# A layer's modulation vectors as fused dot products on VectorE, placed behind SwiGLU blocks

## The chip, the core and the metric

The kernel runs on one core of a Trainium2 chip. A core has five engines that run side by side and wait for each other by semaphores: TensorE (matrix products into PSUM), VectorE (DVE, elementwise work and reductions), ScalarE (ACT, functions and copies), GpSimd (POOL, elementwise work on SBUF) and SyncE (SP), which here issues the transfers from HBM. Each engine takes its instructions strictly in the order in which they stand in its queue. The metric is the time of one execution on the device in microseconds (us); less is better.

## What is computed

The reference is a backbone of two layers over 256 context tokens and 256 latent tokens of width 1024. In both layers a vector of six modulation terms (shift, scale and gate of the mixer and of the feed-forward) scales what goes in and out. It is a product of a weight matrix with the silu of a conditioning vector, once for the context (`c_ctx`) and once for the latents (`c`):

```python
mod_lat = (jax.nn.silu(c) @ ada_w[l] + ada_b[l])[:, None, :]
mod_ctx = (jax.nn.silu(c_ctx) @ ada_w[l] + ada_b[l])[None, None, :]
sh_m, sc_m, g_m, sh_f, sc_f, g_f = jnp.split(mod_lat, N_MOD, axis=-1)
...
hc = modulate(rmsnorm(ctx_s, norm_mix_g[l]), csh_m, csc_m)
yc, hf_c, hb_c = mix(l, hc @ w_in[l], False, None, None)
ctx_s = ctx_s + cg_m * yc
hcf = modulate(rmsnorm(ctx_s, norm_ffn_g[l]), csh_f, csc_f)
ctx_s = ctx_s + cg_f * channel_mix(l, hcf)
```

`mix` is three kinds of sequence mixers (Fourier, Hyena, S5 state space). `channel_mix` is a dense SwiGLU of width 2816 in layer 0, `(silu(h @ w_gate) * (h @ w_up)) @ w_down`, and in layer 1 eight SwiGLU experts of width 3584, of which each token takes two. All is float32.

## The kernel before

The program runs through these stages in order: mixers of layer 0 (to about 295 us); the output projection `outp` with the norm behind it (to about 385 us); the dense feed-forward of layer 0 (to about 800 us); mixers of layer 1; router and experts of layer 1, whose 336 weight loads of 1 MB make up the second half of the time. A scheduler sets each engine's order when the kernel is built, from the order of the code, the dependencies, free buffers and a timing model; nothing is reordered on the chip.

**Modulation (`ada`, L429).** A modulation vector has 6 x 1024 entries, that is 48 columns `m` of 128. Column `m` needs 128 rows of the transposed weights, `ar` (128 x 1024, 512 KB, loaded at L432 from `adaT` into a ring of two buffers), and the row `crow` that holds silu of the conditioning vector on all partitions. The entry is the dot product of the two along the free axis, for `s` = 0 (context) and `s` = 1 (latents). There are two ways: one fused instruction on VectorE (`'v'`, L437, output `jk`, the sum as its accumulator), or a product on GpSimd (`'g'`, L440, into `pd`, one buffer) and a copy with accumulation on ScalarE (L441). When eight columns are there, `mods_done` adds the bias and forms the gains `G` (L384, L387). Columns 0 to 31 of layer 0 are made elsewhere, on TensorE. Columns 32 to 47 of layer 0 are asked for ahead of the output projection (L1155 to L1158): 8 dots on VectorE, 24 on GpSimd and ScalarE. All 48 of layer 1 are asked for by `ahead(fi)` (L1243), eight columns at the end of each feed-forward step, all on GpSimd and ScalarE; from column 16 on only for the latents. That is 88 products on GpSimd and 8 fused dots.

**Weight split (`load` L185, `split` L191, L192).** Every float32 weight block goes into a ring of two buffers `raw`, then into a high half `wh` (copy on ScalarE, L191) and a low half `wl` (difference on VectorE, L192), each 128 x 1024 and in a ring of two. TensorE then does three products a block: high by high, high by low, low by high.

**Feed-forward.** Six steps of up to four blocks of 128 SwiGLU values (22 in all). A block has a gate and an up product of 24 matmuls each, of 512 columns (`pgu`); then silu on ScalarE (L1283), the product `hv` on VectorE (L1285), its high half `HH` on ScalarE (L1286) and its low half `HL` on VectorE (L1287). After the second block of a step the down products of the step before stand (`downs`): eight of up to 12 matmuls into two accumulators `pacc`, each added to the residual stream by two VectorE instructions `xT` of 256 columns (L1227). In steps 1 to 5 `mats1` builds the six sets of S5 matrices of layer 1 by the table `MATS1` (`s5_mats`, L558 and on: products and sums on VectorE and GpSimd, transposes `pbt` on TensorE, stores to HBM), for the mixers of layer 1.

**Output projection.** `outp` (L1161) is eight products whose results `xT` takes up (L1169); the norm sums squares (`nac`, L516), and `put` makes the feed-forward's input in halves `fhH` and `fhL` (L536 to L538).

SP issues all of these loads in one queue; one that waits for a free buffer holds those behind it.

Of the kernel before, what the change touches and what calls it, by code (L numbers as in the profile page):

```python
# [8 lines left out]
F32 = mybir.dt.float32  # L9
F32R = mybir.dt.float32r  # L10
I32 = mybir.dt.int32
AF = mybir.ActivationFunctionType
# [4 lines left out]
D = 1024  # L17
# [8 lines left out]
S5_OFF = 1408  # L26
NHY = [2, 2, 2, 2, 2, 1]
NHY0 = [2,2,2,2,1,2]
MATS1 = [(), (0,), (1,), (2, 3), (4,), (5,)]
HYO = [[10, 2, 3, 4, 5, 6, 7, 8, 9, 0, 1], [2, 3, 4, 5, 6, 7, 8, 9, 10, 0, 1]]  # L30
OW = 5
NRAW = 15
# [103 lines left out]
def build(tc, A, out, dbg=None, upto='all'):  # L136
    nc = tc.nc
    V, S, G, PE, SP = nc.vector, nc.scalar, nc.gpsimd, nc.tensor, nc.sync
    tt_, ts_, stt, act = V.tensor_tensor, V.tensor_scalar, V.scalar_tensor_tensor, S.activation
    gtt = G.tensor_tensor  # L140
    mul, add, sub = OP.mult, OP.add, OP.subtract
# [15 lines left out]
    par = es_par.enter_context(tc.tile_pool(name="par", bufs=1, side="right"))  # L157
# [50 lines left out]
    crow = par.tile([128, 2, D], F32, name="crow")  # L208
# [217 lines left out]
        mods_done(0, 4 * c, 4)  # L426


    def ada(l, m0, m1, eng, pool):  # L429
        for m in range(m0, m1):  # L430
            r = pool.tile([128, D], F32, name="ar", tag="ar", bufs=2)
            SP.dma_start(r, A['adaT'][l, m])  # L432
            for s in range(1 if l == 1 and m >= 16 else 0, 2):
                o = mods[l][:, m, s:s + 1]
                if eng(m, s) == 'v':
                    jk = par.tile([128, D], mybir.dt.bfloat16, name="jk", tag="jk", bufs=1)
                    stt(jk, r, 1.0, crow[:, s], op0=mul, op1=mul, accum_out=o)  # L437
                else:
                    pd = par.tile([128, D], F32, name="pd", tag="pd", bufs=1)
                    gtt(pd, r, crow[:, s], op=mul)  # L440
                    act(pd, pd, AF.Copy, accum_out=o)  # L441
            if m % 8 == 7:
                mods_done(l, m - 7, 8, 1 if l == 1 and m >= 16 else 0)

# [113 lines left out]
    def s5_mats(p, l, q, M, rh, rd):  # L558
# [24 lines left out]
        bh = lambda v: v[:, :, None, :].to_broadcast(sh)  # L583
        for i, (src, op) in enumerate(((bre, sub), (bim, add))):
            tt_(src, bt(PB[0]), bh(bb[:, i]), op=mul)
            (tt_ if l else gtt)(x2, bt(PB[1]), bh(bb[:, 1 - i]), op=mul)
            tt_(src, src, x2, op=op)
            pt = pt_('mat', (128, 4, 128), "pbt")
            for g in range(4):
                PE.transpose(pt[:, g], src[:, g].rearrange("p t h -> p (t h)"), ident)  # L590
            act(M[:, :, 128 * i:128 * i + 128], pt, AF.Copy)
# [535 lines left out]
    with z_es:  # L1127
        yH = z.tile([128, KD, 512], F32R, name="yH", tag="hH")
        yL = z.tile([128, KD, 512], F32R, name="yL", tag="hL")

        with tc.tile_pool(name="z0p", bufs=1) as z2, tc.tile_pool(name="ada0", bufs=1) as p_:
            def fill0(q):
                if q == 0:
                    ada_ring(4, p_)
                if q == 1:
                    ada_ring(5, p_)
                if q == 3:
                    ada_ring(6, p_)
                if q == 4:
                    ada_ring(7, p_)  # L1140
            mixers(0, hH, hL, z2, yH, yL, fill0)
        tap('yH0', yH.bitcast(F32))
        tap('yL0', yL.bitcast(F32))
        rx_es, xp = ExitStack(), ExitStack()
        rx = rx_es.enter_context(tc.tile_pool(name="rx", bufs=1))
        xpool = xp.enter_context(tc.tile_pool(name="xpool", bufs=1))
        xT = xpool.tile([128, KD, 512], F32, name="xT")
        for q in range(4):
            SP.dma_start(xT[:, 2 * q:2 * q + 2], A['xT'][:, 2 * q:2 * q + 2])
        fh = xp.enter_context(tc.tile_pool(name="fh", bufs=1))  # L1150
        fhH, fhL = (fh.tile([128, KD, 512], F32R, name=n_) for n_ in ("fhH", "fhL"))
        ac = rx.tile([128, 2, D], F32, name="nac", tag="xtok")
        nrm = [Norm(0, 1, xT, s, ac[:, s, 0:256]) for s in range(2)]
        apl = xp.enter_context(tc.tile_pool(name="ada1", bufs=1))
        ada(0, 32, 36, lambda m, s: 'gv'[s], apl)  # L1155
        ada(0, 36, 40, lambda m, s: 'gv'[s], apl)
        ada(0, 40, 44, lambda m, s: 'gg'[s], apl)
        ada(0, 44, 48, lambda m, s: 'gg'[s], apl)  # L1158
        with tc.tile_pool(name="ow", bufs=OW) as ow:

            def outp(m, ws, s0, s1):  # L1161
                n = 256 * (s1 - s0)
                cs_ = slice(256 * s0, 256 * s1)
                pa = pacc((128, n))
                for k in (0, 1, 5, 6, 7, 2, 3, 4):
                    mm3(pa, ws[0][:, k], ws[1][:, k], yH[:, k, cs_], yL[:, k, cs_], k == 0, k == 4)
                for s in range(s0, s1):
                    x = xT[:, m, 256 * s:256 * s + 256]
                    stt(x, pa[:, 256 * (s - s0):256 * (s - s0) + 256], mods[0][:, 16 + m, s:s + 1], x, op0=mul, op1=add)  # L1169
                    nrm[s].feed(m)  # L1170
            raws, ws = {}, {}

            def wget(m):
                c = m // 2
                if c not in raws:
                    raws[c] = load(wcols(A['w_out'][0], 256 * c, 256), KD, 256)
                return split(raws[c][:, :, (m % 2) * 128:(m % 2) * 128 + 128], KD, 128,
                             *([ow] if m >= KD - OW else []))
            for m in range(KD - OW):
                outp(m, wget(m), 0, 2)  # L1180
            for m in range(KD - OW, KD):
                ws[m] = wget(m)
                outp(m, ws[m], 0, 1)
            nrm[0].stats()
            nrm[0].put(lambda k: fhH[:, k, 0:256], lambda k: fhL[:, k, 0:256])
            for m in range(KD - OW, KD):
                outp(m, ws[m], 1, 2)
            nrm[1].stats()
            nrm[1].put(lambda k: fhH[:, k, 256:512], lambda k: fhL[:, k, 256:512])
# [10 lines left out]
    with tc.tile_pool(name="ffn", bufs=2, side="right") as fp, banks(gu=3, fk=1):  # L1200
# [9 lines left out]
        def mats1(q):  # L1210
            M = pp1.tile([128, 4, 768], F32, name="M")
            rh = pp1.tile([128, 4, 64], F32, name="rh")
            s5_mats(pp1, 1, q, M, rh, rdr[q])
            SP.dma_start(rhdr[q], rh)
            SP.dma_start(mdr[q][:, :, 0:512], M[:, :, 0:512])
            SP.dma_start(mdr[q][:, :, 640:768], M[:, :, 640:768])
# [23 lines left out]
                        down(g, 4 * dh + 2 * q + m, w, m * 128, 0, 2)  # L1240


        def ahead(fi):  # L1243
            ada(1, 8 * fi, 8 * fi + 8, lambda m, s: 'g', apl)
            for q in MATS1[fi]:
                mats1(q)
        pend = None
        for fi, f0 in enumerate(range(0, nff, 4)):
            nf = min(4, nff - f0)
# [2 lines left out]
            for c in range(0, nf, 2):  # L1252
# [18 lines left out]
                for m in range(2):  # L1271
# [12 lines left out]
                    hv = tmp.tile([128, 512], F32, name="hv", tag="t512b", bufs=2)  # L1284
                    tt_(hv, sg, pp[1], op=mul)  # L1285
                    act(HH[:, c + m], hv, AF.Copy)  # L1286
                    tt_(HL[:, c + m], hv, HH[:, c + m].bitcast(F32), op=sub)  # L1287
                if pend:
                    downs(pend)
                    pend = None  # L1290
            ahead(fi)
            pend = f0, nf, HH, HL

        ac = apl.tile([128, D], F32, name="nac", tag="ar", bufs=2)
# [536 lines left out]
```

## Time and profile before

| | us |
|---|---|
| median of three runs (1838.38 to 1842.83) | 1841.52 |
| the profiled execution | 1841.73 |
| its span, first to last instruction | 1839.8 |
| of it busy: TensorE | 1714.5 (93%) |
| VectorE | 805.9 (44%) |
| GpSimd | 518.4 (28%) |
| ScalarE | 429.4 (23%) |

The profile is of one execution. Its span is 1.9 us short of that execution's time, and the execution is 0.2 us from the median. Busy TensorE includes pipelined matmuls whose ends are modelled, so they overlap: the distance between two starts tells the pace. An idle time is put down to the instruction whose semaphore came last.

### The profile page before, as it was taken

The page shows a single profiled execution, that of the slowest core. Times are in us where ns is not written, and L with a number is a line of the kernel's source. Part 1 is how long each engine was busy: PE and PEld are TensorE (multiplying, and loading weights), DVE is VectorE, ACT ScalarE, POOL GpSimd, SP SyncE. Part 2 cuts the span into 40 slices and gives each one's busy share as a digit, 9 for nine tenths or more (in the row PEclk, how much of TensorE's full clock was granted, in tenths as well). Part 3 has the DMA queues.
Part 4 walks back from the last instruction along what each step waited for, and adds up shares of the span by engine and source line. Part 5 has one row for each costly group of instructions (what it writes and reads, how often), then busy time and mean ns, then how long its engine had stood idle before and what let it go on. Part 6 is the DMA issues. An engine that isn't in the chain of part 4 may idle for free. (4 is left out here: it accounts for less than half of the span.)

```text
span 1839.8 us, 47195 instructions
## 1 busy us (share of the span) xinstructions
PE 1714.5 (93%) x20825; PEld 1193.8 (65%) x20825; DVE 805.9 (44%) x1502; ACT 429.4 (23%) x776; POOL 518.4 (28%) x512
## 2 busy tenths in 40 slices
PE   7988899899998998999998999999999989999984
PEld 4665667867766776788777656666666656666642
DVE  7589968875776667363853001111111101011102
ACT  4332324455444443232231000000000000000001
POOL 5965535567877676000420000000000000000000
PEclk7998999999999999999998999999999999999998
DMA  8244345434557555354649999999999999999994
GB/s 297 87 116 126 94 148 177 144 106 145 168 180 248 190 194 194 120 162 141 191 150 419 405 394 418 419 420 419 419 419 418 419 419 419 418 413 413 412 419 160
DMA packets 145461, 506.80 MB, mean 275 GB/s; under 512 B 18590, under 2 KB 71648, under 8 KB 101216
## 3 DMA queue, kind: packets, MB, share of 16 engines
q1 hardware_dynamic: 145248, 503.70, 72.0%
q8 instruction: 165, 2.70, 0.6%
q14 instruction: 48, 0.39, 0.1%
HBM read 489.34 MB, written 14.32 MB: 274 GB/s over the span
## 5 line engine op out<-in xcount | busy, mean ns | idle before, releaser
L148 PE MATMUL pgu<-raw,xe 128*32 128x256 f32 x9408 | 528.2, 379 | 12.2 <-DMA raw<-in_mwp_dram 11.4
L148 PEld LDWEIGHTS pgu<-raw,xe 128*32 128x32 f32 x9408 | 316.3, 110 | 209.5 <-DMA raw<-in_mwp_dram 15.1
L1652 DVE TENSOR_TENSOR sg<-sg,pgu 128x384 f32<-128x384 f32 (+1 forms) x56 | 28.2, 504 | 629.8 <-ACT sg L1651 629.8
L148 PE MATMUL py<-raw,hT 128*32 128x256 f32 x4704 | 270.0, 379 | 8.3 <-DMA raw<-in_mwp_dram 8.2
L440 POOL TENSOR_TENSOR pd<-ar,crow 128x1024 f32<-128x1024 f32 x88 | 226.6, 2575 | 105.4 <-ACT pd L441 83.9
L1547 POOL TENSOR_TENSOR ob<-ob,fgb 128x512 f32<-128x512 f32 x1 | 1.3, 1262 | 880.4 <-ACT ob L1546 880.4
L148 PEld LDWEIGHTS py<-raw,hT 128*32 128x32 f32 x4704 | 156.0, 110 | 110.4 <-DMA raw<-in_mwp_dram 7.9
L192 DVE TENSOR_TENSOR wl<-raw,wh 128x1024 fp32r<-128x1024 f32 x95 | 169.2, 1783 | 72.4 <-ACT wh L191 70.5
L1651 ACT ACTIVATE sg<-pgu 128x384 f32<-128x384 f32 (+1 forms) x56 | 25.2, 450 | 705.6 <-PE pgu L148 705.6
L148 PE MATMUL pgu<-fhL,wh 128*128 128x512 f32 (+1 forms) x376 | 146.2, 389 | 5.1 <-DVE fhL L538 5.1
L148 PE MATMUL pgu<-fhH,wh 128*128 128x512 f32 (+1 forms) x392 | 147.6, 387 | 1.4 <-ACT sg L1283 0.8
L148 PE MATMUL pgu<-fhH,wl 128*128 128x512 f32 (+1 forms) x360 | 142.1, 396 | 3.3 <-DVE wl L192 3.3
L191 ACT ACTIVATE wh<-raw 128x1024 fp32r<-128x1024 f32 x95 | 99.9, 1054 | 147.1 <-PE pacc L148 67.3
L441 ACT ACTIVATE pd<-pd 128x1024 f32<-128x1024 f32 x88 | 93.0, 1057 | 123.9 <-POOL pd L440 121.1
L148 PE MATMUL pacc<-HH,wh 128*128 128x512 f32 (+1 forms) x192 | 76.8, 401 | 14.2 <-DVE xT L1227 10.0
L148 PEld LDWEIGHTS pgu<-fhL,wh 128*128 128x128 f32 x376 | 72.2, 192 | 22.9 <-DVE fhL L538 6.4
L148 PEld LDWEIGHTS pgu<-fhH,wh 128*128 128x128 f32 x392 | 74.0, 193 | 16.6 <-issue 1.1
L148 PEld LDWEIGHTS pgu<-fhH,wl 128*128 128x128 f32 x360 | 68.1, 189 | 23.0 <-issue 4.7
L148 PE MATMUL pacc<-HL,wh 128*128 128x512 f32 (+1 forms) x192 | 74.6, 389 | 0.0
L148 PE MATMUL pacc<-HH,wl 128*128 128x512 f32 (+1 forms) x192 | 73.7, 390 | 0.3 <-DVE wl L192 0.3
L148 PE MATMUL pacc<-h,wm 128*128 128x256 f32 x272 | 64.5, 391 | 1.2 <-ACT h L549 1.2
L148 PEld LDWEIGHTS pacc<-h,wm 128*128 128x128 f32 x272 | 51.5, 194 | 9.0 <-ACT h L549 1.4
(583 smaller groups left out, 2410.8 us busy)
## 6 DMA issues: line engine op xcount, KB each, us to landing
raw<-in_mwp_dram SPq DMA_DIRECT2D x336, 1024.0 KB
ar<-in_adaT_dram SPq DMA_DIRECT2D x64, 512.0 KB
raw<-in_fwg_dram SPq DMA_DIRECT2D x11, 1024.0 KB
raw<-in_fwu_dram SPq DMA_DIRECT2D x11, 1024.0 KB
raw<-in_fwd_dram SPq DMA_DIRECT2D x11, 1024.0 KB
raw<-in_adaN_dram SPq DMA_DIRECT2D x8, 1024.0 KB
ar<-in_adaN_dram SPq DMA_DIRECT2D x16, 512.0 KB
raw<-in_w_out_dram SPq DMA_DIRECT2D x8, 1024.0 KB
```

The source lines that it names most:

```text
L148: return PE.matmul(o, l, r, start=start, stop=stop, **kw)
L191: act(h, r, AF.Copy)
L192: tt_(l, r, h.bitcast(F32), op=sub)
L440: gtt(pd, r, crow[:, s], op=mul)
L441: act(pd, pd, AF.Copy, accum_out=o)
L1547: gtt(o_, o_, fgb[:, hs], op=mul)
L1651: act(sg[:, 0:n], p[:, 0:n, 0:128], AF.Silu)
L1652: tt_(sg[:, 0:n], sg[:, 0:n], p[:, 0:n, 128:256], op=mul)
```

## The change

All 96 dots now are fused instructions on VectorE; `pd`, its product on GpSimd and its sum on ScalarE are gone. Ahead of the output projection only columns 32 to 39 of layer 0 are left (16 dots). The others go through the list `AHEAD`: 20 entries of four dots (two columns for both `s`, or four columns for the latents), one entry behind each of the first 20 `HL`. `tc.issue_after` gives each dot of an entry an edge from that `HL`, so that VectorE's queue has them behind it; their loads are free of it. `jk` moves to the pool that holds `ar`. In layer 1's matrix building the product `x` (L586) goes from VectorE to GpSimd, as it already stands in layer 0, and `MATS1` moves the fourth matrix (number 3) from step 3 to step 4.

```diff
--- before.py
+++ after.py
@@ -26,7 +26,7 @@
 S5_OFF = 1408
 NHY = [2, 2, 2, 2, 2, 1]
 NHY0 = [2,2,2,2,1,2]
-MATS1 = [(), (0,), (1,), (2, 3), (4,), (5,)]
+MATS1 = [(), (0,), (1,), (2,), (3, 4), (5,)]
 HYO = [[10, 2, 3, 4, 5, 6, 7, 8, 9, 0, 1], [2, 3, 4, 5, 6, 7, 8, 9, 10, 0, 1]]
 OW = 5
 NRAW = 15
@@ -426,19 +426,13 @@
         mods_done(0, 4 * c, 4)
 
 
-    def ada(l, m0, m1, eng, pool):
+    def ada(l, m0, m1, pool):
         for m in range(m0, m1):
             r = pool.tile([128, D], F32, name="ar", tag="ar", bufs=2)
             SP.dma_start(r, A['adaT'][l, m])
             for s in range(1 if l == 1 and m >= 16 else 0, 2):
-                o = mods[l][:, m, s:s + 1]
-                if eng(m, s) == 'v':
-                    jk = par.tile([128, D], mybir.dt.bfloat16, name="jk", tag="jk", bufs=1)
-                    stt(jk, r, 1.0, crow[:, s], op0=mul, op1=mul, accum_out=o)
-                else:
-                    pd = par.tile([128, D], F32, name="pd", tag="pd", bufs=1)
-                    gtt(pd, r, crow[:, s], op=mul)
-                    act(pd, pd, AF.Copy, accum_out=o)
+                jk = pool.tile([128, D], mybir.dt.bfloat16, name="jk", tag="jk", bufs=1)
+                stt(jk, r, 1.0, crow[:, s], op0=mul, op1=mul, accum_out=mods[l][:, m, s:s + 1])
             if m % 8 == 7:
                 mods_done(l, m - 7, 8, 1 if l == 1 and m >= 16 else 0)
 
@@ -583,7 +577,7 @@
         bh = lambda v: v[:, :, None, :].to_broadcast(sh)
         for i, (src, op) in enumerate(((bre, sub), (bim, add))):
             tt_(src, bt(PB[0]), bh(bb[:, i]), op=mul)
-            (tt_ if l else gtt)(x2, bt(PB[1]), bh(bb[:, 1 - i]), op=mul)
+            gtt(x2, bt(PB[1]), bh(bb[:, 1 - i]), op=mul)
             tt_(src, src, x2, op=op)
             pt = pt_('mat', (128, 4, 128), "pbt")
             for g in range(4):
@@ -1152,10 +1146,7 @@
         ac = rx.tile([128, 2, D], F32, name="nac", tag="xtok")
         nrm = [Norm(0, 1, xT, s, ac[:, s, 0:256]) for s in range(2)]
         apl = xp.enter_context(tc.tile_pool(name="ada1", bufs=1))
-        ada(0, 32, 36, lambda m, s: 'gv'[s], apl)
-        ada(0, 36, 40, lambda m, s: 'gv'[s], apl)
-        ada(0, 40, 44, lambda m, s: 'gg'[s], apl)
-        ada(0, 44, 48, lambda m, s: 'gg'[s], apl)
+        ada(0, 32, 40, apl)
         with tc.tile_pool(name="ow", bufs=OW) as ow:
 
             def outp(m, ws, s0, s1):
@@ -1240,10 +1231,14 @@
                         down(g, 4 * dh + 2 * q + m, w, m * 128, 0, 2)
 
 
-        def ahead(fi):
-            ada(1, 8 * fi, 8 * fi + 8, lambda m, s: 'g', apl)
-            for q in MATS1[fi]:
-                mats1(q)
+
+        AHEAD = [(0, m, m + 2) for m in range(40, 48, 2)] + [(1, m, m + 2) for m in range(0, 16, 2)]
+        AHEAD += [(1, m, m + 4) for m in range(16, 48, 4)]
+
+        def ahead(ins):
+            if AHEAD:
+                with tc.issue_after(ins.ins):
+                    ada(*AHEAD.pop(0), apl)
         pend = None
         for fi, f0 in enumerate(range(0, nff, 4)):
             nf = min(4, nff - f0)
@@ -1284,11 +1279,12 @@
                     hv = tmp.tile([128, 512], F32, name="hv", tag="t512b", bufs=2)
                     tt_(hv, sg, pp[1], op=mul)
                     act(HH[:, c + m], hv, AF.Copy)
-                    tt_(HL[:, c + m], hv, HH[:, c + m].bitcast(F32), op=sub)
+                    ahead(tt_(HL[:, c + m], hv, HH[:, c + m].bitcast(F32), op=sub))
                 if pend:
                     downs(pend)
                     pend = None
-            ahead(fi)
+            for q in MATS1[fi]:
+                mats1(q)
             pend = f0, nf, HH, HL
 
         ac = apl.tile([128, D], F32, name="nac", tag="ar", bufs=2)
```

VectorE's queue from the second-last block ahead of a down stage (step 3) into that stage. Before; `HL` ends a block, `wl` is a weight split, `xT` the evictions of down products, `bb`, `u`, `bre` the matrix building:

```order
L1287 TENSOR_TENSOR HL<-hv,HH 128x512
L192 TENSOR_TENSOR wl<-raw,wh 128x1024
L1285 TENSOR_TENSOR hv<-sg,pgu 128x512
L192 TENSOR_TENSOR wl<-raw,wh 128x1024
L1287 TENSOR_TENSOR HL<-hv,HH 128x512
L1227 SCALAR_TENSOR_TENSOR xT<-pacc,mods_100,xT 128x256 x4
L245 TENSOR_TENSOR bb<-u_5919,u_5920 128x64
L246 TENSOR_TENSOR u_5919<-bs,wim 128x64
L247 TENSOR_TENSOR u_5920<-bs,wre 128x64
```

The same place in the change, with its own line numbers:

```order
L1282 TENSOR_TENSOR HL<-hv,HH 128x512
L435 SCALAR_TENSOR_TENSOR jk,mods_101<-ar,crow 128x1024 x2
L192 TENSOR_TENSOR wl<-raw,wh 128x1024
L435 SCALAR_TENSOR_TENSOR jk,mods_101<-ar,crow 128x1024 x2
L1280 TENSOR_TENSOR hv<-sg,pgu 128x512
L192 TENSOR_TENSOR wl<-raw,wh 128x1024
L1282 TENSOR_TENSOR HL<-hv,HH 128x512
L435 SCALAR_TENSOR_TENSOR jk,mods_101<-ar,crow 128x1024
L1218 SCALAR_TENSOR_TENSOR xT<-pacc,mods_100,xT 128x256 x2
L435 SCALAR_TENSOR_TENSOR jk,mods_101<-ar,crow 128x1024
L1218 SCALAR_TENSOR_TENSOR xT<-pacc,mods_100,xT 128x256 x2
L245 TENSOR_TENSOR bb<-u_6320,u_6321 128x64
```

Two dots stand on each side of a weight split inside a block, and in the down stage one dot stands ahead of each pair of evictions.

SP's queue around the down weights of step 4. Before (`ar` are the modulation loads, `md` the stores of built matrices, `cs` and `bs` parameters for them):

```order
L185 DMA raw<-in_fwg_dram 128x8x256
L432 DMA ar<-in_adaT_dram 128x1024
L185 DMA raw<-in_fwu_dram 128x8x256
L432 DMA ar<-in_adaT_dram 128x1024 x3
L567 DMA cs<-in_s5c_dram 128x2x64
L566 DMA bs<-in_s5b_dram 128x2x64
L616 DMA rd_132<-R 4x32x240
L568 DMA d_6451<-in_s5d_dram 128x1x16
L432 DMA ar<-in_adaT_dram 128x1024
L185 DMA raw<-in_fwd_dram 128x4x512
```

In the change:

```order
L185 DMA raw<-in_fwg_dram 128x8x256
L185 DMA raw<-in_fwu_dram 128x8x256
L432 DMA ar<-in_adaT_dram 128x1024 x6
L185 DMA raw<-in_fwd_dram 128x4x512
L432 DMA ar<-in_adaT_dram 128x1024 x2
L185 DMA raw<-in_fwd_dram 128x4x512
L432 DMA ar<-in_adaT_dram 128x1024 x4
L185 DMA raw<-in_fwg_dram 128x8x256
```

Six modulation loads now stand between an up weight and the down weight behind it, where there were four.

## Rows read from the trace of the kernel before

**Rows 1.** Page, part 1: busy us, share of the span, instructions.
```profile
PE 1714.5 (93%) x20825; PEld 1193.8 (65%) x20825; DVE 805.9 (44%) x1502; ACT 429.4 (23%) x776; POOL 518.4 (28%) x512
```

**Rows 2.** Stretches: length, busy us (count) by engine, clock, DMA share, GB/s.
```profile
295.00:385.00 90.00, 76.20 (x494) 68.65 (x494) 80.88 (x122) 47.01 (x84) 48.66 (x19) 0.92 0.51 166
385.00:750.00 365.00, 341.66 (x1621) 258.51 (x1620) 248.73 (x272) 165.53 (x269) 258.05 (x156) 0.97 0.56 181
750.00:830.00 80.00, 78.99 (x431) 63.81 (x430) 40.60 (x91) 26.58 (x47) 0.52 (x1) 0.98 0.48 152
950.00:1840.00 890.00, 844.47 (x15134) 531.46 (x15133) 137.88 (x329) 58.58 (x126) 1.55 (x2) 0.98 0.98 401
```

**Rows 3.** Chain that ended last: start us, us, what (two of its loads).
```profile
950.41 5.20 DMA raw<-in_w_out_dram
...
1797.22 19.66 DMA raw<-in_mwp_dram
```

**Rows 4.** Waits, matmuls in 295 to 385: releaser, us, times, longest.
```profile
PE pgu L148 <- DVE fhL L538: 5.1, 6, 1.4
PE pacc L148 <- DVE xT L1169: 3.3, 2, 2.0
...
PE pacc L148 <- DVE wl L192: 1.7, 1, 1.7
```

**Rows 5.** Waits, matmuls in 385 to 750, whole list.
```profile
PE pacc L148 <- DVE xT L1227: 10.0, 5, 3.8
PE pbt L590 <- DVE bre L587: 5.0, 2, 3.2
PE pacc L148 <- ACT M L591: 4.1, 2, 3.1
PE pgu L148 <- DVE wl L192: 3.3, 3, 1.6
PE pbt L590 <- DVE bim L587: 0.8, 1, 0.8
```

**Rows 6.** Groups of VectorE in 295 to 385: busy us, mean ns, idle before.
```profile
L192 DVE TENSOR_TENSOR wl<-raw,wh 128x1024 fp32r<-128x1024 f32 x10 | 19.3, 1946 | 2.2 <-ACT wh L191 2.2
L538 DVE SCALAR_TENSOR_TENSOR fhL<-nf,mods,fhH 128x256 fp32r<-128x256 f32 x16 | 16.6, 1055 | 0.0
```

**Rows 7.** Groups of VectorE in 385 to 750.
```profile
L192 DVE TENSOR_TENSOR wl<-raw,wh 128x1024 fp32r<-128x1024 f32 x52 | 107.0, 2058 | 49.6 <-ACT wh L191 48.9
...
L1287 DVE TENSOR_TENSOR HL<-hv,HH 128x512 fp32r<-128x512 f32 x18 | 20.4, 1133 | 1.7 <-ACT HH L1286 1.7
...
L586 DVE TENSOR_TENSOR x<-PB,bb 128x512 f32<-128x512 f32 x12 | 11.5, 956 | 0.1
```

**Rows 8.** Groups of VectorE in 750 to 800.
```profile
L192 DVE TENSOR_TENSOR wl<-raw,wh 128x1024 fp32r<-128x1024 f32 x9 | 11.0, 1226 | 12.9 <-ACT wh L191 12.5
L1227 DVE SCALAR_TENSOR_TENSOR xT<-pacc,mods,xT 128x256 f32<-128x256 f32 x8 | 3.5, 480 | 5.8 <-PE pacc L148 5.8
L1287 DVE TENSOR_TENSOR HL<-hv,HH 128x512 fp32r<-128x512 f32 x4 | 2.7, 684 | 0.0
L1285 DVE TENSOR_TENSOR hv<-sg,pgu 128x512 f32<-128x512 f32 x3 | 2.1, 689 | 12.1 <-PE pgu L148 12.1
```

**Rows 9.** Tiles pd and jk: ns min/median/max, first and last start.
```profile
L440 POOL TENSOR_TENSOR pd<-ar,crow x88: 2346/2400/3391, 293.9 to 721.6; 128x1024 f32<-128x1024 f32 x88
...
L437 DVE SCALAR_TENSOR_TENSOR jk<-ar,crow x8: 1208/1213/3053, 293.6 to 331.0; 128x1024 bf16<-128x1024 f32 x8
```

**Rows 10.** Timeline, one product on GpSimd and VectorE's next: start us, us.
```profile
521.53 2.84 POOL L440 TENSOR_TENSOR pd<-ar,crow 128x1024 f32<-128x1024 f32 x1
...
522.04 2.88 DVE L1287 TENSOR_TENSOR HL<-hv,HH 128x512 fp32r<-128x512 f32 x1
```

**Rows 11.** Timeline, TensorE inside a gate product.
```profile
576.70 0.39 PE L148 MATMUL pgu<-fhL,wh 128*128 128x512 f32 x1
...
577.40 0.40 PE L148 MATMUL pgu<-fhL,wh 128*128 128x512 f32 x1
```

## Prediction, written before the change was run

> **What bounds the kernel now.** I read the page first: TensorE is busy 93% of the span, VectorE 44%, GpSimd 28% [rows 1]. Such shares are averages over stages, so the next view is the table of stretches [rows 2]. From 950 us on, the transfers are busy for 0.98 of the time: the experts' weights set the pace there, and the chain that ended last runs through these loads to the end [rows 3]. Nothing in the change touches that part. It ends a fixed time after it starts, so a microsecond saved ahead of it is a microsecond of the result, and none of it is hidden by a later wait.
>
> The change works on two stretches ahead of that. In 295 to 385 us (output projection and the norm behind it) TensorE is busy 76.20 of 90 us at a mean granted clock of 0.92, while VectorE is busy 80.88 [rows 2]. In 385 to 750 us (dense feed-forward) TensorE is busy 341.66 of 365 us at 0.97 [rows 2]. So TensorE bounds both, and what can be won is what it loses there: idle 13.8 and 23.3 us, and clock (1 - 0.92) x 90 = 7.2 and (1 - 0.97) x 365 = 11.0 us. Together that is 55 us. The clock is at its lower level, 1.2 instead of 2.4 GHz, only in short pieces of these stretches.
>
> Next I read who ends TensorE's idle time. In the first stretch VectorE ends 5.1 + 3.3 + 1.7 = 10.1 of the 13.8 us [rows 4]. In the second it is the eviction of the down products (10.0), the matrix building (5.0), a ScalarE copy (4.1) and the low half of a weight split (3.3): 22.4 of 23.3 us [rows 5]. VectorE is not full in the second stretch (248.73 of 365 us, rows 2), so the question is why it is late. The groups of its instructions answer that: the split `wl` takes 2058 ns on average in the feed-forward [rows 7], but 1226 ns in 750 to 800 us, where GpSimd is idle [rows 8, 2]; `HL` takes 1133 against 684 ns [rows 7, 8]. A pair of rows shows the mechanism: GpSimd begins a product `pd` at 521.53 for 2.84 us, VectorE's `HL` begins at 522.04 and lasts 2.88 us instead of 0.68 [rows 10]. A VectorE instruction with two operands in SBUF stands still until GpSimd's product is through. The 88 products `pd` are what GpSimd mostly does [rows 9].
>
> **What is removed.** All 88 products on GpSimd at a median of 2.40 us, and the 88 ScalarE sums behind them [rows 9]. GpSimd's own time is on no path to the end, but its hold on VectorE is. In the feed-forward `wl` gets back 52 x (2058 - 1226) = 43 us and `HL` 18 x (1133 - 684) = 8 us [rows 7, 8]. In the first stretch `wl` gets back 10 x (1946 - 1226) = 7.2 us, and `fhL` 16 x (1055 - 480) = 9.2 us, with the 128x256 form of `xT` as its clean price [rows 6, 8]. The ScalarE sums also go; in the ACT queue they stand ahead of the copies that the weight split and `HH` need, and I take the 4.1 us put down to a ScalarE copy [rows 5] to be of that kind. The twelve `x` products of the matrix building leave VectorE as well (11.5 us, rows 7) and go to GpSimd, at about 1.2 us each (an estimate: half of `pd`'s 2.40 us for half its columns). There they hold VectorE for about 14 us, in place of 88 products of 2.40 us.
>
> **What is added.** 88 more dot products on VectorE. The eight that it already does give the price: 1.21 us at the median, 3.05 at worst behind a GpSimd product [rows 9]. In the first stretch eight more cost 9.7 us, and `wl` and `fhL` alone give back 16.4: VectorE ends 6.7 us lighter there or better. In the feed-forward 80 dots cost 97 us against 43 + 8 + 11.5 = 62.5 from these groups and more from the small ones, so its load stays near 250 to 285 of some 350 us. What changes is where the time stands. Four dots follow one `HL`. A block of SwiGLU values is 48 matmuls, and three matmuls take 0.70 us [rows 11], so a block is 11.2 us; VectorE's work in it is then two `wl` (2.45), `hv` (0.69), `HL` (0.68) and four dots (4.85): 8.7 us [rows 8, 9]. It fits, and the order puts a `wl` between the dots, so in the gate and up blocks I cost the dots at nothing; their cover is the 2.5 us that VectorE has over, and without it each group would cost up to 4.9 us.
>
> In the down stage the cover is thinner. There the order has a dot ahead of the first pair of evictions and another ahead of the second, and the matrix building among them. Two accumulators serve eight down products, so a product waits when the eviction two before it is late by more than its own 2.8 us (12 matmuls). I price a late dot and a late 128x512 instruction, 1.21 + 0.68 [rows 8, 9]: about 2 us for each of the five down stages, 10 us in all. The bound below is nothing, and the bound above is four dots a stage, 24 us.
>
> **The other queues.** The `ar` loads still go through SP in a ring of two, and now wait for dots in place of GpSimd products. Behind them in the same queue stand the weight loads `fwg`, `fwu`, `fwd`, the stores of the built matrices and the small parameter loads. A dot group frees its two buffers within 2.4 us of its start, and a 1 MB load lands in 5.20 us [rows 3]; a block is 11.2 us. So I cost this wait at nothing; the second rival says what it is worth otherwise. `MATS1` builds the fourth matrix one step later, with the fifth; it still ends before the next layer's mixers, nothing.
>
> **The sum.** First stretch: of the 10.1 us that VectorE ends I take back all but 2, since the dots stand in front of the first evictions there: 8, and half of the clock's 7.2, 3.6. That is 11.6 us, between 0 and 21. Feed-forward: 22.4 us of named waits go and 10 come, a gain of 12.4 us; idle time falls from 23.3 to 10.9 us, and with the clock's loss in proportion (11.0 to 5.2) there are 5.8 more. That is 18.2 us, between 0 and 34. The profiled execution took 1841.73 us (span 1839.8), level with the median of 1841.52: 1841.7 - 11.6 - 18.2 = 1811.9, so **1812 us**.
>
> **Rivals.** *All of it goes*: no dot is ever in the way, and 55.3 us vanish: 1786 us. The 8.7 of 11.2 us speak for it, the evictions behind dots against it. Chance 0.12.
>
> *Half of it*: the first stretch gains its 11.6 us, and in the feed-forward the dots in front of evictions and splits cost as much as the GpSimd products did: 1830 us. For it speaks that VectorE's load there hardly falls. Chance 0.16.
>
> *Nothing*: this happens as well, and in the first stretch the 16 dots wait in VectorE's queue for their `ar` loads, with splits and evictions behind them: 1841 us. Chance 0.08.
>
> *Slower, by the load queue*: in the later steps up to six `ar` loads stand in SP between one weight load and the next, and each waits for a dot that itself waits for an `HL`. If in each of ten half steps one weight load is late by a landing of 5.20 us [rows 3], that adds 52 us: 1864 us. It decides from 3 us per half step, where the 30 us gained are gone. Against it: before, the same ring waited for GpSimd with the same loads behind, and no weight load of the feed-forward is among TensorE's releasers [rows 5]. Chance 0.09.
>
> *Slower, by a dot at half rate*: if a dot with its accumulator took twice the 1.21 us, a block would need 3.8 + 9.7 = 13.5 us of VectorE for 11.2 of TensorE, and 20 blocks x 2.3 = 47 us would come on top: 1859 us. The eight rows at 1.21 us, level with `wl` at 1.23 for as many elements, speak against it [rows 8, 9]; they ran apart, not four in a row. Chance 0.03. The Trainium skill (Vector Engine (DVE) Microarchitecture Reference, Points that are easy to get wrong) has this as a rule: a scalar_tensor_tensor with two SBUF sources that are not bf16 runs at half its throughput, as no read port is left for the accumulator. By that rule the dots would bind as this rival says; the trace of before does not agree with it.
>
> **How the numbers follow.** The forecast, 1800 to 1824 us, has 0.52. This kernel's measurement can tell some 0.3%, 5.5 us, from no change. Faster by more than that (under 1836): 0.52 + 0.12 + 0.16 = 0.80; within: 0.08; slower: 0.09 + 0.03 = 0.12. The range of 1795 to 1840 us leaves out the slower cases (0.12), the upper part of no change (0.03) and the lower half of the largest gain (0.05).
>
> **What would show it.** In the profile of after, `pd` is gone from GpSimd and ScalarE, 96 dots stand on VectorE near 1.21 us, and `wl` in the feed-forward falls to 1.4 us or less. TensorE's idle time in the first stretch is about 5 us, and in the feed-forward about 11, put down mostly to `xT`. The first expert loads are issued some 30 us earlier, and the stretch from there to the end is as long as before. I am wrong if TensorE waits for `wl` or `fwd` behind dots, if the dots take 2.4 us, or if splits stay at 2 us with GpSimd nearly empty.

## The result: 1808.9 us against 1842.1

The changed kernel takes 1808.9 us at the median (1806.2 to 1812.1) where the kernel before takes 1842.1 (1838.4 to 1842.8): a ratio of 0.9827, 95% interval 0.9812 to 0.9843. Beside the last experiments it was measured again: 1811.4 us, 0.9834 (0.9819 to 0.9850). The forecast was 1812. The profiled execution took 1806.2 us (span 1804.3); it is the fastest of its four, so the spans lie 35.5 us apart and the medians 33.2.

Part 1 of the page after, to be held against [rows 1]. The columns are the same.

```profile
PE 1698.4 (94%) x20825; PEld 1185.1 (66%) x20825; DVE 810.6 (45%) x1666; ACT 334.9 (19%) x600; POOL 313.2 (17%) x436
```

GpSimd has lost 205 us of work, ScalarE 94 us, and VectorE, which took over 88 dots, is only 5 us busier. That the shares say little more than this is why the stretches come next. First the two fixed windows of [rows 2]:

```profile
295.00:385.00 90.00, 85.62 (x558) 77.04 (x556) 73.30 (x159) 32.52 (x55) 0.00 (x0) 0.98 0.48 158
385.00:750.00 365.00, 352.00 (x1693) 268.42 (x1692) 269.95 (x406) 93.67 (x133) 104.49 (x98) 0.99 0.57 189
```

These windows hold later work than before, since everything has moved forward. A fair comparison cuts at the same events: the first output product, the first `HL`, the last down product. The same view, cut there; the kernel before:

```profile
292.84:387.80 94.96, 81.16 (x515) 72.38 (x514) 85.12 (x125) 50.36 (x89) 52.21 (x21) 0.93 0.52 172
387.80:822.20 434.40, 410.71 (x2001) 313.93 (x2000) 280.47 (x336) 184.16 (x298) 256.51 (x155) 0.98 0.53 172
```

And after:

```profile
290.94:370.20 79.26, 73.39 (x504) 66.98 (x503) 62.79 (x140) 30.07 (x51) 0.94 (x1) 0.98 0.50 166
370.20:787.50 417.30, 403.97 (x2010) 311.47 (x2010) 307.76 (x486) 109.60 (x160) 104.49 (x98) 0.99 0.57 187
```

The output projection with the norm and the first block is 15.7 us shorter, the rest of the feed-forward 17.1. Together that is 32.8 of the 35.5 us between the two spans. In these two stretches TensorE's idle time falls from 13.8 + 23.7 = 37.5 to 5.9 + 13.3 = 19.2 us. For the clock the means of this view are too coarse (0.01 of the second stretch is 4 us); the trace itself has the granted clock at its lower level, 1.2 GHz, for 13.7 + 20.5 us before and for 1.9 + 8.3 us after. Reckoned as half of such time, the loss falls from 17.1 to 5.1 us. Idle time and clock together explain 18.3 + 12.0 = 30.3 us. The other 2.5 lie inside TensorE's busy time, whose matmuls overlap with modelled ends; no view here splits them further. A second trace of the change (e12 below) has 79.1 and 420.8 us for the two stretches, with 17.8 us of idle time and 8.5 of clock won: the feed-forward's gain is 14 to 17 us, and the clock's part differs from one execution to the next.

What follows is untouched. The chain that ended last has the load of [rows 3] at

```profile
914.35 5.11 DMA raw<-in_w_out_dram
```

instead of 950.41: 36 us earlier. From there to the end of the span it is 889.9 us, before 889.4. (This load is a weight of layer 1's output projection; the first load of the experts is issued at 888.9 us instead of 925.3.) The saving passed through whole.

Who ends TensorE's idle time after the change (waits of its matmuls: releaser, us, times, longest). First 290.94 to 370.20, the three longest, to be held against [rows 4]:

```profile
PE pacc L148 <- DVE xT L1160: 2.6, 2, 1.7
PE pacc L148 <- DVE yL L972: 1.5, 1, 1.5
PE pgu L148 <- DVE fhL L532: 0.8, 1, 0.8
```

Then 370.20 to 787.50, the whole list, against [rows 5]:

```profile
PE pgu L148 <- DVE wl L192: 6.0, 4, 3.7
PE pbt L584 <- DVE bre L581: 3.7, 3, 2.0
PE pacc L148 <- DVE xT L1218: 3.3, 4, 1.6
PE pacc L148 <- DVE wl L192: 0.3, 1, 0.3
```

The ScalarE copy `M` is gone from the list, `fhL` has shrunk from 5.1 to 0.8 us and `xT` of the down products from 10.0 to 3.3. The split `wl` has grown, from 3.3 to 6.0.

The groups of VectorE after, 385 to 720 us, against [rows 7]:

```profile
L435 DVE SCALAR_TENSOR_TENSOR jk<-ar,crow 128x1024 bf16<-128x1024 f32 x67 | 87.5, 1306 | 4.8 <-DMA ar<-in_adaT_dram 3.9
L192 DVE TENSOR_TENSOR wl<-raw,wh 128x1024 fp32r<-128x1024 f32 x50 | 63.1, 1261 | 25.5 <-ACT wh L191 24.1
...
L1282 DVE TENSOR_TENSOR HL<-hv,HH 128x512 fp32r<-128x512 f32 x17 | 11.6, 684 | 0.0
```

And 295 to 375 us, against [rows 6]:

```profile
L192 DVE TENSOR_TENSOR wl<-raw,wh 128x1024 fp32r<-128x1024 f32 x10 | 12.1, 1219 | 6.3 <-ACT wh L191 6.3
...
L532 DVE SCALAR_TENSOR_TENSOR fhL<-nf,mods,fhH 128x256 fp32r<-128x256 f32 x16 | 7.0, 477 | 0.0
```

The same instructions on the same operands: `wl` 1261 ns instead of 2058, `HL` 684 instead of 1133, `fhL` 477 instead of 1055. Each is within 3% of its price in the stretch in which GpSimd is idle: 1226, 684, and 480 for the 128x256 form [rows 8].

### The profile page after: what moved, and what is told of

Its sections match the earlier page's. It is cut to its first block, busy times and chain, and to the rows that moved or that the text cites. A ratio compares the mean times of both kernels' runs of the same rounds, so it can differ in the third digit from the quotient of the medians.

```text
span 1804.3 us, 47096 instructions
## 1 busy us (share of the span) xinstructions
PE 1698.4 (94%) x20825; PEld 1185.1 (66%) x20825; DVE 810.6 (45%) x1666; ACT 334.9 (19%) x600; POOL 313.2 (17%) x436
## 5 line engine op out<-in xcount | busy, mean ns | idle before, releaser
L192 DVE TENSOR_TENSOR wl<-raw,wh 128x1024 fp32r<-128x1024 f32 x95 | 124.8, 1316 | 40.2 <-ACT wh L191 37.7
L435 DVE SCALAR_TENSOR_TENSOR jk<-ar,crow 128x1024 bf16<-128x1024 f32 x96 | 124.5, 1297 | 8.2 <-DMA ar<-in_adaT_dram 7.2
L1218 DVE SCALAR_TENSOR_TENSOR xT<-pacc,mods,xT 128x256 f32<-128x256 f32 x96 | 42.3, 477 | 26.7 <-PE pacc L148 26.5
```

Source lines behind the costliest of these rows:

```text
L192: tt_(l, r, h.bitcast(F32), op=sub)
L435: stt(jk, r, 1.0, crow[:, s], op0=mul, op1=mul, accum_out=mods[l][:, m, s:s + 1])
```

## Experiments

Two theories stood at the start. **H**: VectorE is held by GpSimd's products. **S**: what costs is the 88 sums in ScalarE's queue, ahead of the copies of the weight split. All ratios are against the kernel before on the same chip.

**The products alone left out** (e1), then **the sums alone left out** (e2).

```diff
@@ e1: before, without the product @@
-                    gtt(pd, r, crow[:, s], op=mul)
-                    act(pd, pd, AF.Copy, accum_out=o)
+                    act(pd, r, AF.Copy, accum_out=o)
@@ e2: before, without the sum; mods preset to 0 at the start @@
                     gtt(pd, r, crow[:, s], op=mul)
-                    act(pd, pd, AF.Copy, accum_out=o)
```

> The kernel before, with the 88 GpSimd products left out: the ScalarE sum reads the load itself (so these modulation entries are sums of a weight row, without the conditioning vector). The 88 sums of about 1.25 us stay on ScalarE, GpSimd keeps only its other work, VectorE keeps its eight dots. Theory H (VectorE is held by GpSimd's products): nearly all of the change's 33 us comes from this, 1800 to 1815 us, wl in the feed-forward at 1.4 us or less, TensorE's waits for xT, bre and wl mostly gone. Theory S (what costs is the 88 sums in ScalarE's queue, each with copies for the weight split behind it): the sums still take their 110 us there, only their wait for GpSimd goes; half of the gain at most, 1820 to 1835 us.

> The kernel before, with the 88 ScalarE sums left out and the products kept (the entries are preset to zero, once, at the start). ScalarE loses the sums and the wait for GpSimd in its queue (121 us of idle time before the sums by the waits of ScalarE). GpSimd's 88 products of 2.40 us stay, with the same hold on VectorE, only sooner. Theory H: little changes, 1832 to 1845 us, wl in the stretches with products still near 2 us, TensorE still waits for xT and wl. Theory S: most of the gain, 1808 to 1820 us.

Measured: e1 1815.0 us, 0.9851 (0.9827 to 0.9874). e2 1870.8 us, 1.0156 (1.0131 to 1.0182): slower than the kernel before. In e1 `wl` takes 1318 ns in 385 to 750 us. TensorE now waits longer for ScalarE at three places (`fhH`, `wh` and `sg` had 0.5, nothing and 0.8 us before); waits of its matmuls in 285 to 830 us:

```profile
PE pgu L148 <- ACT fhH L536: 4.8, 1, 4.8
PE pacc L148 <- DVE xT L1226: 4.0, 5, 1.6
PE pacc L148 <- ACT wh L191: 3.8, 1, 3.8
PE pgu L148 <- ACT sg L1282: 2.1, 1, 2.1
```

The products alone are worth 27 us, with the sums still there: H holds, at the upper edge of its range. The sums are not free either. Their products gone, they run earlier and wait for their loads: the longest wait, 4.8 us for `fhH`, ends just behind a sum for whose load ScalarE had been idle for 7.04 us. A run further down, e4, has neither products nor sums and dots of almost no length; it takes 1800.0 us, 15 less than e1. That bounds what S is worth beside H, but does not price it, since other places in the queues differ too.

e1 also takes away ScalarE's waits for the products (121 us of its idle time before), which might have been the cause in place of VectorE's. In e2 these waits are gone as well and nothing is gained, which speaks against that. The 4.1 us that TensorE waited for the ScalarE copy `M` are gone in e1 although the sums stayed.

e2 missed its range, 1832 to 1845, and the miss is instructive. GpSimd's timeline in e2 (start, us, idle before it and what ended that):

```profile
319.77 5.69 POOL L442 TENSOR_TENSOR pd<-ar,crow 128x1024 f32<-128x1024 f32 x2 [3.19 <-DMA ar<-in_adaT_dram]
330.42 2.46 POOL L442 TENSOR_TENSOR pd<-ar,crow 128x1024 f32<-128x1024 f32 x1 [4.96 <-DMA ar<-in_adaT_dram]
333.23 13.23 POOL L442 TENSOR_TENSOR pd<-ar,crow 128x1024 f32<-128x1024 f32 x5 [0.35 <-DMA ar<-in_adaT_dram]
```

The same engine in the kernel before:

```profile
336.37 2.39 POOL L440 TENSOR_TENSOR pd<-ar,crow 128x1024 f32<-128x1024 f32 x1 [1.26 <-ACT pd L441]
340.02 2.40 POOL L440 TENSOR_TENSOR pd<-ar,crow 128x1024 f32<-128x1024 f32 x1 [1.26 <-ACT pd L441]
```

Before, the one buffer `pd` made each product wait 1.26 us or more for the sum behind it, and in that gap VectorE had its turn. Without the sum, products run in a row, and the last row of e2 goes on past the window shown: ten products from 333.23 to 358.79 us. Beside these ten stands the iteration for the norm's inverse root on VectorE, a chain of instructions of 0.16 us each. In e2 about every second one takes 1.6 to 2.3 us instead, as if it got its turn only between two products, and the chain lasts 14.6 us; it lasts 6.9 in the kernel before and 4.0 after the change. From first output product to first `HL` it now takes 120 us instead of 95, at a lower clock:

```profile
290.90:411.00 120.10, 85.94 (x501) 76.75 (x500) 105.29 (x124) 29.85 (x51) 74.60 (x29) 0.82 0.44 144
```

So the products seem to be worse the denser they come, and ScalarE's sum to have been a brake on them. That the gap is the reason was read from the timelines, not tried by itself: the scheduler orders both kernels' queues anew, and 28 of the 88 products now start in this stretch, where there were 20. The Trainium skill (SBUF — State Buffer, Who interferes with whom) states the rule behind H: of the engines only VectorE and GpSimd contend, by an exclusive lock on a shared pair of ports, and "Issue order, not op shape, decides who blocks." The traces agree, with 2.88 us for an `HL` of 0.68 behind a product begun 0.51 us earlier [rows 8, 10].

**One part alone**: the output projection's (e3), the feed-forward's (e9).

```diff
@@ e3: before, ahead of the output projection @@
-        ada(0, 32, 36, lambda m, s: 'gv'[s], apl)
-        ada(0, 36, 40, lambda m, s: 'gv'[s], apl)
-        ada(0, 40, 44, lambda m, s: 'gg'[s], apl)
-        ada(0, 44, 48, lambda m, s: 'gg'[s], apl)
+        ada(0, 32, 40, lambda m, s: 'v', apl)
...
         def ahead(fi):
+            if fi == 0:
+                ada(0, 40, 48, lambda m, s: 'g', apl)
@@ e9: after, with both ways in ada @@
-        ada(0, 32, 40, apl)
+        ada(0, 32, 40, apl, lambda m, s: 'gv'[s])
+        ada(0, 40, 48, apl, lambda m, s: 'g')
...
-        AHEAD = [(0, m, m + 2) for m in range(40, 48, 2)] + [(1, m, m + 2) for m in range(0, 16, 2)]
+        AHEAD = [(1, m, m + 2) for m in range(0, 16, 2)]
```

> The kernel before with only the part of the change ahead of the output projection: columns 32 to 39 of layer 0 as 16 fused dots, columns 40 to 47 moved to the first step of the feed-forward, as GpSimd products with ScalarE sums like those of layer 1 there. From the two traces the first stretch (first output product to the first HL) is 15.7 us shorter after the change. Theory: these 15.7 us come whole from the 24 products that are gone from it, and the feed-forward is unchanged but for 16 more products in its first step, which cost 0 to 4 us: 1826 to 1832 us. Rival: the first stretch is shorter because of what the change does elsewhere (earlier loads), then 1838 us or more.

> The counterpart of e3_wout_only: ahead of the output projection as before (8 dots, 24 GpSimd products with ScalarE sums), and the feed-forward as changed, with the 64 dots of layer 1 in 16 groups behind the first 16 HL. e3 gained 2 us where 12 to 16 were expected, by the trace since about half of the products were still in the first stretch and the rest cost in the feed-forward what they had cost before. If products cost where they run, this kernel loses only what the first stretch had won, 15.7 us from first output product to first HL: 1809 + 16 = 1825 us, 1820 to 1831. If the two parts only work together: 1835 us or more.

Measured: e3 1839.5 us, 0.9981 (0.9966 to 0.9995); e9 1829.0 us, 0.9928 (0.9910 to 0.9945). e3 is a miss. In it only 8 of 24 products have become dots; the other 16 are moved, and the scheduler starts them early. The tile `pd` of e3 in 290 to 390 us (ns min/median/max, first and last start):

```profile
L440 POOL TENSOR_TENSOR pd<-ar,crow x11: 2363/2403/3012, 338.2 to 384.7; 128x1024 f32<-128x1024 f32 x11
```

Eleven products are still in the first stretch, where there were 20. By the trace (of the longest of its ten executions) that stretch, 295.51 to 384.8 us, is 5.7 us shorter than before, and the feed-forward behind it, to 825.7, is 6.5 longer. Moving a product moves its hold; only taking it away gains. e9 confirms it from the other side: with 24 products left ahead of the output projection its first stretch is as long as before (94.8 us, first `HL` at 387.4; before, 95.0 and 387.8), its feed-forward is 12.3 us shorter than before, and it is 18 to 20 us behind the change, as expected.

**The price of the dots**: cut to 16 columns (e4), done twice (e5).

```diff
@@ e4 @@
-                stt(jk, r, 1.0, crow[:, s], op0=mul, op1=mul, accum_out=mods[l][:, m, s:s + 1])
+                n = D if l == 0 and m < 40 else 16
+                stt(jk[:, 0:n], r[:, 0:n], 1.0, crow[:, s, 0:n], op0=mul, op1=mul, accum_out=mods[l][:, m, s:s + 1])
@@ e5 @@
+                for _ in range(1 if l == 0 and m < 40 else 2):
```

> The changed kernel with the 80 dots of the feed-forward cut to the first 16 of 1024 columns (these entries then lack the rest of the sum): same loads, same places in the queues, almost no VectorE time. It prices the dots. The prediction had them at nothing in the gate and up blocks and at about 10 us with the clock's part in the down stages. If that holds: 1796 to 1803 us. If the dots are free throughout: 1806 to 1809 us. If the dots push the splits in the gate and up blocks as well: 1790 us or less.

> The changed kernel with each of the 80 dots of the feed-forward done twice, one behind the other (the second writes the same entry). It tests the cover: by the prediction a block of 11.2 us has 8.7 us of VectorE work with four dots, so 2.5 us are over, and four more dots (4.85 us) should push each of 20 blocks by some 2.4 us: 1809 + 47 = 1856 us, 1840 to 1870. Rival: cover is not per block, and VectorE catches up in the following blocks and down stages; by the whole feed-forward it is busy 270 of 365 us, so 97 us more would fit but for a few us: 1815 to 1830 us.

Measured: e4 1800.0 us, 0.9767 (0.9744 to 0.9789); e5 1822.5 us, 0.9887 (0.9859 to 0.9916). The 80 dots cost 9 to 12 us, by medians or by ratios, and as many again 10 to 14 more, not the 47 of the first expectation. Waits of TensorE's matmuls in e4, 371 to 780 us:

```profile
PE pacc L148 <- DVE xT L1219: 3.6, 2, 1.9
PE pbt L585 <- DVE bim L582: 0.5, 1, 0.5
PE pacc L148 <- DVE wl L192: 0.3, 1, 0.3
```

The wait for `xT` is the same 3.6 us as with whole dots (3.3); what the dots add is the waits for `wl` and `bre`, 6.3 + 3.7 us against 0.3 and 0.5 (for `bim`) in e4. In e5, 385 to 750 us, VectorE is busy 344 of 365 us:

```profile
385.00:750.00 365.00, 340.00 (x1673) 259.05 (x1674) 344.08 (x532) 90.36 (x130) 120.40 (x98) 0.98 0.57 183
```

With so little idle time left the kernel still beats the one before, but by its first stretch alone: its feed-forward, 369.8 to 805.3 us, takes 435.5 us, as long as the 434.4 before. What it did not lose are the 47 us of a budget per block. The rival expectation fits, by which VectorE is late in one block and catches up in the next.

**Where the dots stand** (e8, without the edge from `HL`).

```diff
-                with tc.issue_after(ins.ins):
-                    ada(*AHEAD.pop(0), apl)
+                ada(*AHEAD.pop(0), apl)
```

> The changed kernel without the edge from HL: the same dots, asked for at the same places in the code, but the scheduler puts them where its model likes, which is early: all 80 stand in VectorE's queue before the second half of the feed-forward, up to nine between one HL and the next, and 14 in a row behind the norm. No GpSimd product either way. Theory H says that the gain comes from the products' going, so that most of it stays: 1808 to 1822 us. Rival, placement is what matters: the dots wait in VectorE's queue for their loads ahead of splits and evictions, and the gain is gone: 1830 us or more.

Measured: 1840.7 us, 0.9984 (0.9972 to 0.9995). It has no product `pd`, and the gain is gone: H forecast 1808 to 1822 us here and missed, and the rival, that placement decides, held. TensorE's waits in 285 to 830 us begin with

```profile
PE pbc L148 <- DVE ny L457: 15.3, 2, 10.5
PE pgu L148 <- DVE wl L192: 7.8, 4, 4.0
```

and VectorE's timeline shows why (`nt` and `ny` are links of the iteration for the norm's inverse root, on two columns each):

```profile
361.84 1.23 DVE L435 SCALAR_TENSOR_TENSOR jk<-ar,crow 128x1024 bf16<-128x1024 f32 x1
362.99 0.08 DVE L435 DVE_READ_ACCUMULATOR jk<-ar,crow 128x1 f32 x1
362.99 0.16 DVE L457 SCALAR_TENSOR_TENSOR ny<-nt,nj 128x2 f32<-128x2 f32 x1
364.00 1.23 DVE L435 SCALAR_TENSOR_TENSOR jk<-ar,crow 128x1024 bf16<-128x1024 f32 x1 [0.85 <-DMA ar<-in_adaT_dram]
365.15 0.08 DVE L435 DVE_READ_ACCUMULATOR jk<-ar,crow 128x1 f32 x1
365.15 0.16 DVE L455 TENSOR_TENSOR nt<-ny 128x2 f32<-128x2 f32 x1
```

Between two links of 0.16 us stands a dot of 1.23 us, and ahead of it at times a wait for its load. The links of this chain start 1.57 us apart, in the change 0.20: a chain that TensorE waits for has become some eight times as long. The first `HL` of e8 comes at 393.4 us, that of the change at 370.2.

**The small parts**: `x` of the matrix building back on VectorE (e6), the old table of the matrices (e7).

```diff
@@ e6 @@
-            gtt(x2, bt(PB[1]), bh(bb[:, 1 - i]), op=mul)
+            (tt_ if l else gtt)(x2, bt(PB[1]), bh(bb[:, 1 - i]), op=mul)
@@ e7 @@
-MATS1 = [(), (0,), (1,), (2,), (3, 4), (5,)]
+MATS1 = [(), (0,), (1,), (2, 3), (4,), (5,)]
```

> The changed kernel with the twelve x products of layer 1's matrix building back on VectorE (as before), all else as changed. On GpSimd they hold VectorE (x there takes 1.0 to 2.0 us, and dots beside them 1.6 to 2.1 us instead of 1.21); on VectorE they cost 12 x 0.68 = 8 us. If the hold costs as much as the work: 1806 to 1812 us, no difference. If GpSimd's x is a real relief of VectorE: slower, 1813 to 1818 us. If the hold is dearer: 1800 to 1805 us.

> The changed kernel with the old table for the matrix building: the fourth matrix in step 3 together with the third, the fifth alone in step 4. The prediction costed the move at nothing: 1806 to 1812 us. Rival: with two matrices in step 3 the down stage there is late, 1813 to 1820 us.

Measured: e6 1809.7 us, 0.9810 (0.9785 to 0.9835); e7 1814.0 us, 0.9837 (0.9817 to 0.9858). Neither can be told from the change by its ratio (0.9827 and 0.9834), though the 1814.0 us of e7 lie in the range of its rival. In the change `x` on GpSimd holds VectorE about as long as the work that it takes from it: VectorE is busy 810.6 us in the change and 810.9 with the twelve `x` on it (e6). The group on GpSimd in 385 to 720 us:

```profile
L580 POOL TENSOR_TENSOR x<-PB,bb 128x512 f32<-128x512 f32 x10 | 13.2, 1320 | 7.5 <-DVE bre L581 6.8 <-DVE bb L248 0.7
```

**A candidate** without dots ahead of the down evictions of steps 2 to 4 (e10), and with `x` on VectorE as well (e11), beside the change itself (e12).

```diff
-        AHEAD += [(1, m, m + 4) for m in range(16, 48, 4)]
+        AHEAD += [(1, m, min(m + 5, 48)) for m in (16, 21, 26, 31)] + [(1, 36, 40), (1, 40, 44), (1, 44, 48)]
...
-                    ahead(tt_(HL[:, c + m], hv, HH[:, c + m].bitcast(F32), op=sub))
+                    hl = tt_(HL[:, c + m], hv, HH[:, c + m].bitcast(F32), op=sub)
+                    if fi not in (2, 3, 4) or c + m != 1:
+                        ahead(hl)
```

> A candidate: the changed kernel without dots ahead of the down evictions of steps 2 to 4. Those three HL get no group; the 20 groups become 19 (four latent groups have five columns) and move on by up to three blocks. e4 says all 80 dots cost about 9 us, and what is left of TensorE's waits for xT and wl in the feed-forward is 7.5 us. If the late evictions are what the dots cost: 1802 to 1806 us. If the loss just moves to the splits of the blocks that get the groups: 1807 to 1811 us.

> The same candidate with the twelve x products on VectorE as well. e6 found no difference from that alone, so the same as e10 to within 3 us; with VectorE free of dots in the down stages and of GpSimd's hold at the matrix building, 1800 to 1805 us at best.

> The changed kernel unaltered, beside the candidates on the same chip: 1806 to 1812 us.

Measured: 1812.3 us, 0.9843 (0.9826 to 0.9860); 1811.2 us, 0.9835 (0.9819 to 0.9852); and the change 1811.4 us, 0.9834. No difference. In e10 TensorE still waits 5.3 us for `xT` of the down products, not less than in the change (3.3 and, in e12, 3.6): the loss moves, as the second expectation of e10 had it. No version that does all of the work can be told to beat the change.

## Why the prediction came out

**The bound.** That a microsecond saved ahead of the experts' loads is one of the result held to half a microsecond (889.4 and 889.9 us from the load of the chain to the end). The load of [rows 3] at 950.41 us is not yet one of the experts', but they follow it in the chain.

**What is removed.** The mechanism was right and carries the result: e1 has 27 us from the products alone, and `wl`, `HL` and `fhL` fell to the prices of [rows 8]. What the text left out is that a product may cost by how close it follows the last: by the timelines of e2 the sum behind it was also a brake. And products going was not enough: without the edge from `HL` (e8) nothing was gained in all. The 4.1 us of `M` it laid to the sums; they went in e1, where the sums stayed, so if that queue was the cause, it was the sums' wait for the products.

**The sum.** The forecast took back 8 + 12.4 = 20.4 us of idle time and 3.6 + 5.8 = 9.4 us of clock, 29.8 in all. Cut at the same events the traces have 18.3 and 12.0 us, and 2.5 more inside TensorE's busy time (e12: 17.8 and 8.5, and 3.1). In the first stretch the idle term was right (7.9 measured, 8 forecast), the clock's undersized (5.9 measured, 3.6 forecast). In the feed-forward the idle term was 2 too large (10.4 measured, 12.4 forecast), and the clock's, 5.8, lies between the 6.1 and 2.6 of the two traces. That the total fits better than its parts is partly luck.

**What is added.** Here a right number stood in the wrong place. The prediction put 10 us on late evictions in the down stages and nothing on the gate and up blocks. The dots do cost 9 to 12 us (e4), but through `wl` and the matrix building; `xT` waits as long with short dots as with whole ones, and e10, which clears three of the five down stages, gains nothing. That the two came to the same 10 us is luck. The budget of a block, 8.7 of 11.2 us, left out the matrix building that runs in the blocks between two steps. The longest wait after the change, 3.7 us for a `wl`, ends at 507 us among four dots and nine small products of that kind.

**The cover.** It was said to be 2.5 us a block, with up to 4.9 us a group lost without it. e5 took it away and lost 0.5 to 0.7 us a group, as if VectorE's slack were shared over blocks.

**The rivals.** *All of it goes* is bounded by e4, at 1800 us even with the dots nearly free: 1786 was out of reach by this change. *By the load queue* did not happen: no load is among TensorE's releasers in the feed-forward after the change. (That a group frees its two buffers within 2.4 us holds for the eight groups of the latents alone; the other twelve have two dots a buffer and need 4 x 1.21 = 4.8 us.) *A dot at half rate*: the 96 dots have a median of 1223 ns, level with `wl` at 1219. The Trainium skill's rule on this (Vector Engine (DVE) Microarchitecture Reference, Points that are easy to get wrong) is not borne out in a row either: three that follow each other directly in the change (from 649.82 us) and four in e5 (from 407.06) take 1.22 to 1.23 us each. And by e5, which doubles the dots' time, such a rate would have given 1822 us, not 1859: that rival was overpriced by the same budget per block. *Nothing*, with dots waiting for loads ahead of what TensorE needs, has the time of e8, 1840.7 us against 1841, but only in part its cause: in e8 dots stand in the norm's chain, the first stretch (292.21 to 393.4 us) is some 6 us longer than before and the feed-forward some 9 shorter. In the change the edge from `HL` keeps the dots out of such places, and the gain rests on it as much as on the products' going.

**What would show it.** `wl` at 1261 ns (1400 or less), idle 4.4 us in the first window (about 5) and 13.0 in the second (about 11), the experts' loads 36 us earlier (some 30): much as said. "Put down mostly to `xT`" was wrong: `wl` leads. And one of the signs by which the prediction would be wrong did show, TensorE waiting for `wl` behind dots, for 6.0 us in all; so most of the cost was found in the gate and up blocks, where the prediction had put nothing.

## What to carry to other kernels

An engine that is idle is not free: before giving GpSimd side work, look whether VectorE's two-operand instructions take longer beside it than where GpSimd rests, for that difference is the price. Filler work in an in-order queue needs a place of its own, behind an instruction after which nothing urgent is due; left to float, it falls between the links of a short chain. Slack of an engine need not be reckoned block by block: here a block with more work than time cost 0.5 to 0.7 us, not the 2.3 that it lacked.

## What the hardware showed that was not expected

Taking 88 sums from ScalarE made the kernel slower: 88 products on GpSimd with a gap of 1.26 us or more behind each gave 1842 us, the same 88 with up to ten in a row 1871. That the missing gap is the cause is a reading of the timelines. And VectorE at 344 of 365 us busy (e5) cost the kernel only some 10 to 14 us against 270 of 365: a high share by itself did not bind.
